# A third quad per gate/up block, silu in one ScalarE pass, and turned blocks carried by DMA in an RWKV-7 macaron block

## The chip, the core and the metric

The kernel runs on one core of one Trainium2 chip. A core has TensorE (PE in the profile; its weight loads are PEld), VectorE (DVE), ScalarE (ACT), GpSimd (POOL) and SyncE (SP), each with a queue of its own that it works through in order, and 16 DMA engines. The metric is the time on the device of one execution, in microseconds; before the change it is 2059.87 us, the median of three runs (2057.18 to 2060.95).

## The reference

One block on 256 tokens of width 2048, in float32: a gated feed-forward network (FFN), a mixer, a second FFN, each with a norm before and after and a residual. The change lies in the two FFNs; of the mixer only that it lies between them matters here.

```python
D_MODEL = 2048
SEQ = 256
D_FF = int(math.ceil(8 * D_MODEL / 3 / 256)) * 256      # 5632
MACARON_WEIGHT = 0.5
...
def _swiglu(x, w_gate, w_up, w_down):
    return (jax.nn.silu(x @ w_gate) * (x @ w_up)) @ w_down
...
    for l in range(DEPTH):
        f = _swiglu(_rmsnorm(h, ln_ffn1_pre[l]), ffn1_gate[l], ffn1_up[l], ffn1_down[l])
        h = h + MACARON_WEIGHT * _rmsnorm(f, ln_ffn1_post[l])
        mx = _hybrid_mixer(_rmsnorm(h, ln_mix_pre[l]), w_in[l], rwkv_mu[l], rwkv_w0[l],
...
        h = h + _rmsnorm(mx, ln_mix_post[l])
        f = _swiglu(_rmsnorm(h, ln_ffn2_pre[l]), ffn2_gate[l], ffn2_up[l], ffn2_down[l])
        h = h + MACARON_WEIGHT * _rmsnorm(f, ln_ffn2_post[l])
```

## The kernel before

*Products in two parts.* TensorE multiplies in a rounded float32 (F32R). To keep float32's accuracy every operand is split into a high part (the rounded value) and a low part (the rest), and a product is three matmuls into one PSUM bank: high x high, low x high, high x low (`mm3`, L173 to L175). Weights come as 128 x 1024 tiles `w32` by SP's DMAs; ScalarE's cast makes the high part `wH` (L149, in quads L379), VectorE's subtraction the low part `wL` (L150, in quads L380). There are four buffers for `w32` (`W32_BUFS`) and five for each of `wH` and `wL` (`WS_BUFS`): a split waits for TensorE to be through with the fifth tile before it, and a load for the splits of the fourth tile before it.

*Tiles.* The 256 tokens are two halves of 128 rows. Gate and up are computed in 11 blocks of 512 columns; each sums over 2048 inputs, 16 slices of 128 called k, two of which make a k pair. A pair of one weight is 4 products, 12 matmuls of 512 columns. Down has four blocks of 512 columns over 44 k.

*Quads.* Blocks 2 to 10 of each FFN (`FAST`) and down use `seven`. It takes two weights together: with the token halves as rows, the two slices of a k pair in the middle and the two weights (gate and up; in down two column blocks) as columns, a k pair is a 2 x 2 by 2 x 2 block product of 8 products. A quad forms it with seven, from sums of inputs (`sums`, made once per FFN as soon as the inputs stand) and from sums of weights that VectorE makes for each quad: `t13` (two differences, L367), then `t24` (L372 and L373, each reading the one before). Four splits follow: `a` and `b` of loaded tiles, `t13`, and `t24`; `a`, `t13` and `t24` hold two products each, `b` one. Before the change two of the eight k pairs of a fast block are quads (`n` = 2, after the fifth gate pair and the second up pair: `((4,), (1,))`), the other six are plain pairs for gate and for up. When the last quad is done, `merge` adds its banks up in VectorE (a copy on ScalarE, L401, and six additions, L404).

*Gate and up together.* `ev_f` then has ScalarE form the sigmoid of the gate's result u into a PSUM bank that has come free (L636), and VectorE multiply u by it (L638): that is silu. At the end of a block `finish` (L414) adds the up result of one half, `ev_l` (L642) multiplies it with the silu, and `turn` (L568) transposes it in VectorE in 32 x 32 squares into a tile `T1`; then the same for the other half. In the plain blocks 0 and 1 `ev_g` and `ev_gm` do silu by a sigmoid and a VectorE product (L653).

*Carrying a turned block.* Down needs the hidden values with the columns on the partitions. The transposed squares must still move between groups of 32 partitions: `carry_at` does that in the next block with 16 ScalarE copies of 32 x 256 (L594), 0.9 us apart on the clock of the hand-written order, and splits the result into high (L598) and low parts (L602).

*The order.* ScalarE, VectorE and TensorE run in an order written out by hand: `put` appends TensorE's steps with their length on a model clock, and `at` sets other work at a time of that clock; `slot` gives the time when one of the five split buffers comes free. What stands in a queue is not overtaken: an operation that waits holds up all behind it. SP and POOL take their instructions as the scheduler places them.

Of the kernel before, what the change touches and what calls it, by code (L numbers as in the profile page):

```python
# [18 lines left out]
P = 128  # L19
D = 2048  # L20
S = 256
# [27 lines left out]
FAST = range(2, 11)  # L49

# [5 lines left out]
class Block:  # L56
# [195 lines left out]
    def sums(s, T, out, when, own=None):  # L252
# [6 lines left out]
        def first():  # L259
            xH, xL = T[len(out) // 2]  # L260
            x = tt["x"] = s.unit((P, 2, 2, S), F32, "sx")
            V.tensor_tensor(out=fl(x), in0=xH.bitcast(F32).rearrange("p k t -> p (k t)"),
                            in1=xL.bitcast(F32).rearrange("p k t -> p (k t)"), op=ALU.add)

        def second():
            x = tt["x"]
            a11, a21 = x[:, :, 0, :P], x[:, :, 0, P:]
            a12, a22 = x[:, :, 1, :P], x[:, :, 1, P:]
            f = tt["f"] = s.unit((P, 4, 2, P), F32, "sf")
# [32 lines left out]
        def third():  # L302
            tt["H"], tt["L"] = [s.unit((P, 4, 2, P), F32R, n_) for n_ in ("sH", "sL")]
            nc.scalar.copy(fl(tt["H"]), fl(tt["f"]))

        def fourth():
            f, fH, fL = tt["f"], tt["H"], tt["L"]
            V.tensor_tensor(out=fl(fL), in0=fl(f), in1=fl(fH).bitcast(F32), op=ALU.subtract)
            for i in range(2):
                out.append([(fH[:, m, i], fL[:, m, i]) for m in range(4)])  # L310
# [4 lines left out]
    def seven(s, wf, cf, wl, cl, at, KT, T, sm, n, spots, ev_first, ev_last, trail=False):  # L315
# [35 lines left out]
        def quad(q):  # L351
# [18 lines left out]
            def t24():  # L370
                o = v["t24"]
                V.tensor_tensor(out=o[:, 0], in0=v["a"][:, 0], in1=v["t13"][:, 1], op=ALU.add)  # L372
                V.tensor_tensor(out=o[:, 1], in0=v["b"][:, 0], in1=o[:, 0], op=ALU.subtract)  # L373
# [22 lines left out]
        def merge():  # L396
# [12 lines left out]
            s.at(m + 4, lambda: ev_first(0, u[1], bank["p1"]))  # L409
            s.at(m + 4.6, lambda: ev_first(1, u[3], bank["p6"]))  # L410

        def finish(h):
            o = u[2 * h]
            V.tensor_tensor(out=o, in0=bank[f"l{h}"], in1=o, op=ALU.add)  # L414
            ev_last(h, o)
# [10 lines left out]
        if trail:  # L426
            s.by_half(wl, cl, stop, KT, s.clk, AHEAD[0],
                      lambda k, h: mul(f"l{h}", rows(k, h), ws[k]), keep, finish)
            return
# [136 lines left out]
    def turn(s, T1, h, src):  # L566

        s.nc.vector.transpose(out=T1[:, h * 512:h * 512 + 512], in_=src)  # L568

    def shuffle_split(s, T1, T, j):  # L570

        nc = s.nc
        x32 = s.unit((P, 4, S), F32, "x32")
        src = T1.rearrange("p (h k j c) -> p h k j c", h=2, k=4, j=4)
        dst = x32.rearrange("p k (h i c) -> p h k i c", h=2, i=4)
        for i in range(4):
            for q in range(4):
                nc.scalar.copy(dst[q * 32:q * 32 + 32, :, :, i],
                               src[i * 32:i * 32 + 32, :, :, q])
        dH, dL = T[j]  # L580
        nc.scalar.copy(dH, x32)
        nc.vector.tensor_tensor(out=dL, in0=x32, in1=dH.bitcast(F32), op=ALU.subtract)

    def carry_at(s, T1, T, t):
# [4 lines left out]
        def one(i, q):  # L589
            src = T1[0].rearrange("p (h k j c) -> p h k j c", h=2, k=4, j=4)  # L590
            if not x:
                x.append(s.unit((P, 4, S), F32, "x32"))
            dst = x[0].rearrange("p k (h i c) -> p h k i c", h=2, i=4)
            nc.scalar.copy(dst[q * 32:q * 32 + 32, :, :, i], src[i * 32:i * 32 + 32, :, :, q])  # L594

        def high():
            T.extend(s.new_T(1))
            nc.scalar.copy(T[-1][0], x[0])  # L598

        def low():  # L600
            dH, dL = T[-1]
            nc.vector.tensor_tensor(out=dL, in0=x[0], in1=dH.bitcast(F32), op=ALU.subtract)  # L602
# [8 lines left out]
    def ffn(s, wg, wu, wd, uT, rs, gpost, resid, emit, reload, xs=None):  # L611
# [7 lines left out]
        def block(b):  # L619
# [8 lines left out]
            def ev_g(h, ps):  # L628
                sg = s.tmp("sg")
                nc.scalar.activation(out=sg, in_=ps, func=AF.Sigmoid, scale=rs[h])  # L630
                nc.vector.scalar_tensor_tensor(out=sg, in0=ps, scalar=rs[h], in1=sg,
                                               op0=ALU.mult, op1=ALU.mult)
                sig[h] = sg

            def ev_f(h, u, free):
                nc.scalar.activation(out=free, in_=u, func=AF.Sigmoid)  # L636
                sig[h] = u
                s.at(s.now + 1.2, lambda: nc.vector.tensor_tensor(  # L638
                    out=u, in0=u, in1=free, op=ALU.mult))

            def ev_l(h, o):
                nc.vector.tensor_tensor(out=o, in0=o, in1=sig[h], op=ALU.mult)  # L642
                turned(h, o)

            def ev_gm(h, ps):
                sg = s.tmp("sg")
                nc.scalar.activation(out=sg, in_=ps, func=AF.Sigmoid, scale=r[h])
                sig[h] = sg
                s.at(s.now + 1.2, lambda: nc.vector.scalar_tensor_tensor(
                    out=sg, in0=ps, scalar=r[h], in1=sg, op0=ALU.mult, op1=ALU.mult))  # L650
# [27 lines left out]
            s.gemm_at(wg, b * 512, x, NKD, ev_gm)  # L678
# [40 lines left out]
    def post(s, wd, at, KT, gpost, fac, resid, emit, reload, hT=None, sm=None):  # L719
# [52 lines left out]
        if hT is not None:  # L772
# [3 lines left out]
            for c in (0, 2):  # L776
                ev = ev_of(c)
                s.seven(wd, c * 512, wd, c * 512 + 512, at, KT, hT, sm, NQ[c == 2], QUADS[c == 2],
                        lambda h, u, _, ev=ev: ev(h, u), ev_of(c + 1), c == 2)
# [761 lines left out]
```

## Time and profile before

| | us |
|---|---|
| median of three runs | 2059.87 |
| lowest and highest | 2057.18, 2060.95 |
| the profiled execution | 2060.43 |
| its span, first to last instruction | 2058.7 |
| TensorE busy in the span | 2043.5 |
| VectorE busy | 1687.5 |
| ScalarE busy | 1247.4 |
| POOL busy | 76.0 |

The blocks are found by the transposes of L568, two per block: those of the first FFN's blocks start between 58.2 and 485.0 us, those of the second's between 1398.6 and 1824.3. The second FFN's down projection follows to the end; between the first FFN's down projection and 1398.6 lie the mixer and the second FFN's first block.

How to read the rows: "busy" is the union of an engine's instructions; the number in brackets is their count. A row of the timeline has the start, the length, engine, line, operation and shapes, a count when like instructions are merged, and in brackets the idle time before it with what ended it. Rows of grouped instructions have the count, the busy time, the mean of one in nanoseconds, and the idle time before them. A matmul's length in the trace overlaps the next one's; its pace is read from start to start.

### The profile page before, as it was taken

Reading aid. Unit: us, or ns where it says so; the run is one execution under the profiler, and the core shown is the slowest. Engines: PE = TensorE matmul, PEld = TensorE weight load, DVE = VectorE, ACT = ScalarE, POOL = GpSimd, SP = SyncE. Lnnn points to the kernel's source line nnn. Section 1 sums busy time; section 2 is a strip of 40 time slices with the busy share of each in tenths; the row PEclk is TensorE's granted clock in tenths of the full one; section 3 lists DMA queues with packets and bytes.
Section 4 is the critical chain, followed back from the end, with each engine's and each line's share of the span. In section 5 each row is a group of like instructions: output and inputs, shape, how many; then the busy total and the mean of one; then the engine's idle time right before and its main releaser. Section 6 shows DMA issues by size and latency. Waiting matters only on the chain.

```text
span 2058.7 us, 29579 instructions
## 1 busy us (share of the span) xinstructions
PE 2043.5 (99%) x10901; PEld 1721.7 (84%) x10901; DVE 1687.5 (82%) x2188; ACT 1247.4 (61%) x1788; POOL 76.0 (4%) x161
## 2 busy tenths in 40 slices
PE   9999999999999999999999999999999999999998
PEld 7888888888888899999888888888888888888886
DVE  6898889888988865799688667578988898889886
ACT  7667666776555574474465444466677666765553
POOL 0000000000000000000110110010000000000000
PEclk9999999999999999999999999999999999999999
DMA  7566666665667766656456565665666666656674
GB/s 259 175 195 211 194 206 194 196 212 176 210 208 251 228 189 187 180 159 196 133 155 193 161 245 189 205 211 169 203 199 200 214 195 194 197 186 215 210 254 155
DMA packets 226170, 407.03 MB, mean 198 GB/s; under 512 B 15199, under 2 KB 51177, under 8 KB 226025
## 3 DMA queue, kind: packets, MB, share of 16 engines
q1 hardware_dynamic: 219849, 384.69, 59.7%
q0 software_dynamic: 5888, 19.93, 2.7%
q8 instruction: 85, 1.39, 0.3%
q10 hardware_dynamic: 288, 0.52, 0.1%
q14 instruction: 60, 0.49, 0.1%
HBM read 396.69 MB, written 8.39 MB: 197 GB/s over the span
## 4 chain that ended last, share of the span: by engine, by line
PE 92%; DVE 3%; issue 2%; DMA 2%; ACT 1%; POOL 0%; POOLq 0%; DVEq 0%; SPq 0%; ACTq 0%
PE mm L173 24%; PE mm L175 23%; PE mm L174 23%; PE mc L523 10%; PE ms L175 3%; PE ms L173 3%; PE ms L174 3%; DMA w<-in_ffn_down_dram 1%; DVE wL L150 1%; PE tr L551 1%; ACT x L594 0%; PE pA L1262 0%; ACT wH L149 0%; DVE u L404 0%; ACT wH L379 0%
## 5 line engine op out<-in xcount | busy, mean ns | idle before, releaser
L150 DVE TENSOR_TENSOR wL<-w,wH 128x1024 fp32r<-128x1024 f32 (+2 forms) x597 | 711.4, 1206 | 232.9 <-ACT wH L149 229.9
L149 ACT CAST wH<-w 128x1024 fp32r<-128x1024 f32 (+2 forms) x597 | 614.8, 1043 | 392.4 <-PE mm L175 200.5
L173 PE MATMUL mm<-wH,xH 128*128 128x512 f32 x2076 | 811.6, 392 | 0.0
L175 PE MATMUL mm<-wH,xL 128*128 128x512 f32 x2076 | 808.5, 389 | 0.7 <-DVE xL L559 0.5
L174 PE MATMUL mm<-wL,xH 128*128 128x512 f32 x2076 | 808.4, 389 | 0.7 <-DVE wL L150 0.7
L175 PEld LDWEIGHTS mm<-wH,xL 128*128 128x128 f32 x2076 | 389.7, 188 | 82.8 <-DVE xL L559 1.5
L174 PEld LDWEIGHTS mm<-wL,xH 128*128 128x128 f32 x2076 | 389.8, 188 | 81.2 <-DVE wL L150 1.6
L173 PEld LDWEIGHTS mm<-wH,xH 128*128 128x128 f32 x2076 | 389.6, 188 | 81.0 <-ACT xH L557 0.2
L379 ACT CAST wH<-t 128x1024 fp32r<-128x1024 f32 x128 | 134.5, 1052 | 72.7 <-DVE t L367 42.6
L380 DVE TENSOR_TENSOR wL<-t,wH 128x1024 fp32r<-128x1024 f32 x128 | 152.5, 1218 | 25.0 <-ACT wH L379 25.0
L379 ACT CAST wH<-w 128x1024 fp32r<-128x1024 f32 (+1 forms) x128 | 107.2, 838 | 96.7 <-PE mm L175 51.6
L523 PE MATMUL mc<-xH,wH 128*128 128x256 f32 x560 | 159.5, 285 | 0.0
L523 PE MATMUL mc<-xL,wH 128*128 128x256 f32 x560 | 158.4, 283 | 0.0
L523 PE MATMUL mc<-xH,wL 128*128 128x256 f32 x560 | 158.4, 283 | 0.0
L594 ACT COPY x<-T 32x256 f32<-32x256 f32 x352 | 142.2, 404 | 10.9 <-DVE T L568 4.6
L380 DVE TENSOR_TENSOR wL<-w,wH 128x1024 fp32r<-128x1024 f32 (+1 forms) x128 | 116.7, 950 | 1.3 <-ACT wH L379 1.3
L523 PEld LDWEIGHTS mc<-xH,wH 128*128 128x128 f32 x560 | 106.0, 189 | 1.1
L523 PEld LDWEIGHTS mc<-xH,wL 128*128 128x128 f32 x560 | 106.0, 189 | 0.2
L523 PEld LDWEIGHTS mc<-xL,wH 128*128 128x128 f32 x560 | 106.0, 189 | 0.1
L367 DVE TENSOR_TENSOR t<-w,w 128x1024 f32<-128x1024 f32 x64 | 78.0, 1218 | 16.4 <-DMA w<-in_ffn_down_dram 12.0
L174 PE MATMUL ms<-wL,sH 128*128 128x512 f32 x164 | 63.8, 389 | 0.0
L175 PE MATMUL ms<-wH,sL 128*128 128x512 f32 x164 | 63.8, 389 | 0.0
(298 smaller groups left out, 1974.7 us busy)
## 6 DMA issues: line engine op xcount, KB each, us to landing
w<-in_ffn_up_dram SPq DMA_DIRECT2D x140, 512.0 KB
w<-in_ffn_gate_dram SPq DMA_DIRECT2D x138, 512.0 KB
w<-in_w_in_dram SPq DMA_DIRECT2D x128, 512.0 KB
w<-in_ffn_down_dram SPq DMA_DIRECT2D x120, 512.0 KB
w<-in_ffn_down_dram SPq DMA_DIRECT2D x112, 256.0 KB
w<-in_ffn_gate_dram SPq DMA_DIRECT2D x76, 256.0 KB
w<-in_ffn_up_dram SPq DMA_DIRECT2D x72, 256.0 KB
w<-in_w_out_dram SPq DMA_DIRECT2D x32, 512.0 KB
```

The lines of the kernel that those rows point to most:

```text
L149: s.nc.scalar.copy(vH, v)
L150: s.nc.vector.tensor_tensor(out=vL, in0=v, in1=vH.bitcast(F32), op=ALU.subtract)
L173: nc.tensor.matmul(ps, aH, bH, start=start, stop=False)
L174: nc.tensor.matmul(ps, aH, bL, start=False, stop=False)
L175: nc.tensor.matmul(ps, aL, bH, start=False, stop=stop)
L367: V.tensor_tensor(out=v["t13"], in0=v["a"], in1=v["b0"].to_broadcast([P, 2, 512]), op=ALU.subtract)
L379: nc.scalar.copy(H, v[n_])
L380: V.tensor_tensor(out=L, in0=v[n_], in1=H.bitcast(F32), op=ALU.subtract)
L523: s.nc.tensor.matmul(o, lh, rh, start=one and n == 0, stop=k == KT - 1 and n == 2, skip_group_check=True)
L551: nc.tensor.transpose(ps[:, i], src[:, i * P:(i + 1) * P], s.ident)
L594: nc.scalar.copy(dst[q * 32:q * 32 + 32, :, :, i], src[i * 32:i * 32 + 32, :, :, q])
```

## The change

- `NG, SPOTS`: a fast block has three quads, after the third and fifth gate pairs and after the second up pair, and five plain pairs for each of gate and up. The sums of inputs for the third k pair are formed in block 1 (`nq=1`, both parts in one tile).
- In every quad, down's too, `t24` is two separate operations: `split("a")` comes between `t13` and the first, `split("b")` between the first and the second.
- In `merge` the order of the six additions changes by one place; at the end of a fast block (`one_end`) both totals, both products and both transposes stand in that order, no longer one half after the other.
- Silu is one ScalarE pass (`AF.Silu`), in place in fast blocks and from PSUM in blocks 0 and 1; the VectorE products are gone.
- `turn` writes its squares in another order, so that `carry_at` can move each of 16 pieces as 32 runs of 1 KB: 16 DMAs issued by POOL take the place of the 16 copies. The splits are made in two halves, the first cast 10 us after the carry's time, the second 13 (`CARRY`), each low part 2 us later.

```diff
+CARRY = (10, 13)
+NG, SPOTS = 3, ((2, 4), (1,))
...
-    def sums(s, T, out, when, own=None):
+    def sums(s, T, out, when, own=None, nq=2):
...
-            xH, xL = T[len(out) // 2]
-            x = tt["x"] = s.unit((P, 2, 2, S), F32, "sx")
-            V.tensor_tensor(out=fl(x), in0=xH.bitcast(F32).rearrange("p k t -> p (k t)"),
-                            in1=xL.bitcast(F32).rearrange("p k t -> p (k t)"), op=ALU.add)
+            xH, xL = [t[:, :2 * nq].bitcast(F32).rearrange("p k t -> p (k t)")
+                      for t in T[len(out) // 2]]
+            x = tt["x"] = s.unit((P, 2, 2, S), F32, "sx")[:, :nq]
+            V.tensor_tensor(out=fl(x), in0=xH, in1=xL, op=ALU.add)
...
-            tt["H"], tt["L"] = [s.unit((P, 4, 2, P), F32R, n_) for n_ in ("sH", "sL")]
+            if nq == 1:
+                u = s.unit((P, 2, 4, 1, P), F32R, "sHL")
+                tt["H"], tt["L"] = u[:, 0], u[:, 1]
+            else:
+                tt["H"], tt["L"] = [s.unit((P, 4, nq, P), F32R, n_) for n_ in ("sH", "sL")]
...
-            def t24():
-                o = v["t24"]
-                V.tensor_tensor(out=o[:, 0], in0=v["a"][:, 0], in1=v["t13"][:, 1], op=ALU.add)
-                V.tensor_tensor(out=o[:, 1], in0=v["b"][:, 0], in1=o[:, 0], op=ALU.subtract)
+            def t2():
+                V.tensor_tensor(out=v["t24"][:, 0], in0=v["a"][:, 0], in1=v["t13"][:, 1],
+                                op=ALU.add)
+
+            def t4():
+                V.tensor_tensor(out=v["t24"][:, 1], in0=v["b"][:, 0], in1=v["t24"][:, 0],
+                                op=ALU.subtract)
...
-            for t, fn in ((a, get), (a, t13), (a, t24), (a, lambda: split("a", 2)),
-                          (b, lambda: split("b", 1)), (c, lambda: split("t13", 2)),
+            for t, fn in ((a, get), (a, t13), (a, lambda: split("a", 2)), (a, t2),
+                          (b, lambda: split("b", 1)), (b, t4), (c, lambda: split("t13", 2)),
                           (d, lambda: split("t24", 2))):
...
-            for j, a in enumerate(((1, "p6", 0), (2, "p7", 1), (3, "p5", 2), (1, "p5", 1),
+            for j, a in enumerate(((1, "p6", 0), (2, "p7", 1), (1, "p5", 1), (3, "p5", 2),
                                    (1, "f0", 1), (3, "f1", 3))):
...
+        def total(h):
+            V.tensor_tensor(out=u[2 * h], in0=bank[f"l{h}"], in1=u[2 * h], op=ALU.add)
...
+        def both():
+            total(0)
+            total(1)
+            ev_last((u[0], u[2]))
...
-        s.nc.vector.transpose(out=T1[:, h * 512:h * 512 + 512], in_=src)
+        dst = T1.rearrange("p (j h k c) -> p h k j c", j=4, h=2, k=4)[:, h]
+        s.nc.vector.transpose(out=dst, in_=src.rearrange("p (k j c) -> p k j c", k=4, j=4))
...
-            nc.scalar.copy(dst[q * 32:q * 32 + 32, :, :, i], src[i * 32:i * 32 + 32, :, :, q])
...
+            x.append(s.unit((P, 4, 2, 4, 32), F32, "x32"))
+            src = T1[0].rearrange("p (j h k c) -> p j h k c", j=4, h=2, k=4)
+            for i in range(4):
+                for q in range(4):
+                    nc.gpsimd.dma_start(out=x[0][q * 32:q * 32 + 32, i],
+                                        in_=src[i * 32:i * 32 + 32, q])
...
-        for n in range(16):
-            s.at(t + 0.9 * n, lambda n=n: one(n // 4, n % 4))
-        s.at(t + 15, high)
-        s.at(t + 17, low)
+        s.at(t, move)
+        for h in range(2):
+            s.at(t + CARRY[h], lambda h=h: high(h))
+            s.at(t + CARRY[h] + 2, lambda h=h: low(h))
...
-            def ev_f(h, u, free):
-                nc.scalar.activation(out=free, in_=u, func=AF.Sigmoid)
+            def ev_f(h, u):
                 sig[h] = u
-                s.at(s.now + 1.2, lambda: nc.vector.tensor_tensor(
-                    out=u, in0=u, in1=free, op=ALU.mult))
-
-            def ev_l(h, o):
-                nc.vector.tensor_tensor(out=o, in0=o, in1=sig[h], op=ALU.mult)
-                turned(h, o)
...
+                nc.scalar.activation(out=u, in_=u, func=AF.Silu)
+
+            def ev_l(o):
+                for h in range(2):
+                    nc.vector.tensor_tensor(out=o[h], in0=o[h], in1=sig[h], op=ALU.mult)
+                for h in range(2):
+                    turned(h, o[h])
...
+                s.sums(st["nT"], st["su"], s.clk + 27, nq=1)
...
-                s.seven(wg, b * 512, wu, b * 512, s.T_at(nT), NKD, nT, su, 2, ((4,), (1,)),
-                        ev_f, ev_l)
+                s.seven(wg, b * 512, wu, b * 512, s.T_at(nT), NKD, nT, su, NG, SPOTS,
+                        ev_f, ev_l, one_end=True)
```

More of the change, by code (lines that the diff above doesn't have):

```diff
@@ L308, in fourth @@
             V.tensor_tensor(out=fl(fL), in0=fl(f), in1=fl(fH).bitcast(F32), op=ALU.subtract)
-            for i in range(2):
+            for i in range(nq):
                 out.append([(fH[:, m, i], fL[:, m, i]) for m in range(4)])
@@ L587, in carry_at, with move, by_k, part @@
         x = []
[L589 to L600, printed above, removed]
[L601 to L606 removed]
+        def move():
+            x.append(s.unit((P, 4, 2, 4, 32), F32, "x32"))
[4 more added lines that the diff above has]
+                                        in_=src[i * 32:i * 32 + 32, q])
+        def by_k(h):
+            return x[0][:, :, h].rearrange("p i k c -> p k i c")
+        def part(t_, h):
+            return t_[:, :, h * P:h * P + P].rearrange("p k (i c) -> p k i c", i=4)
+        def high(h):
+            if h == 0:
+                T.extend(s.new_T(1))
+            nc.scalar.copy(part(T[-1][0], h), by_k(h))
+        def low(h):
+            dH, dL = T[-1]
+            nc.vector.tensor_tensor(out=part(dL, h), in0=by_k(h),
+                                    in1=part(dH, h).bitcast(F32), op=ALU.subtract)
+        s.at(t, move)
+        for h in range(2):
+            s.at(t + CARRY[h], lambda h=h: high(h))
+            s.at(t + CARRY[h] + 2, lambda h=h: low(h))
     def sumsq(s, src, acc):
```

46 lines of the change are left out of this document (14 added, 32 removed).

## The prediction

> **What bounds the kernel now.** I read the totals and the chain that ended last first, then busy time by stage.
>
> ```profile
> span 2058.7 us, 29579 instructions
> PE 2043.5 (99%) x10901; PEld 1721.7 (84%) x10901; DVE 1687.5 (82%) x2188; ACT 1247.4 (61%) x1788; POOL 76.0 (4%) x161
> PE 92%; DVE 3%; issue 2%; DMA 2%; ACT 1%; POOL 0%; POOLq 0%; DVEq 0%; SPq 0%; ACTq 0%
> ```
>
> TensorE is the bound. A busy TensorE may still run slowly, so the stages matter. The first row below holds the gate/up blocks 1 to 10 of the first FFN, the second one fast block, the third the first down projection.
>
> ```profile
> core 0: us, PE busy (x) PEld busy (x) DVE busy (x) ACT busy (x) POOL busy (x), PEclk, DMA share, GB/s
> 101.00:482.00 381.00, 381.00 (x1683) 315.48 (x1682) 336.97 (x370) 261.68 (x362) 0.00 (x0) 1.00 0.63 200
> 225.20:267.40 42.20, 42.20 (x188) 34.95 (x187) 37.43 (x43) 28.96 (x40) 0.00 (x0) 1.00 0.63 200
> 483.00:700.00 217.00, 215.75 (x948) 177.25 (x947) 190.59 (x216) 124.74 (x153) 3.40 (x6) 1.00 0.68 218
> ```
>
> In the gate/up stage TensorE has no idle time at all, at clock 1.00; VectorE is busy 37.43 of 42.20 us (89%), ScalarE 28.96 (69%). Down loses 217.00 - 215.75 = 1.25 us. The pace of a matmul comes from the timeline of TensorE inside that block:
>
> ```profile
> 249.77 0.39 PE L173 MATMUL mm<-wH,xH 128*128 128x512 f32 x1
> ...
> 255.89 0.39 PE L173 MATMUL mm<-wH,xH 128*128 128x512 f32 x1
> ```
>
> From the first row to the last are 27 starts, across pairs and a quad alike: 6.12 / 27 = 0.2267 us each (the 0.39 is latency). So a block is 186 of these, and only fewer matmuls, or a new stall, change it.
>
> **The change, part by part.**
>
> *The third quad.* A quad makes seven products of three matmuls where two pairs make eight: 3 matmuls fewer in each of 18 blocks (9 per FFN), 54 x 0.2267 = **12.2 us**, if nothing starves TensorE. A block becomes 183 matmuls, 41.5 us. The price lies on VectorE, whose own pace the next view shows (the block's end; TensorE enters the next block at 267.45).
>
> ```profile
> 260.49 2.73 DVE L404 TENSOR_TENSOR u<-ms,u 128x512 f32<-128x512 f32 x4
> 263.26 1.29 DVE L404 TENSOR_TENSOR u<-mm,u 128x512 f32<-128x512 f32 x2
> 264.46 1.22 DVE L150 TENSOR_TENSOR wL<-w,wH 128x1024 fp32r<-128x1024 f32 x1
> 266.18 1.23 DVE L150 TENSOR_TENSOR wL<-w,wH 128x1024 fp32r<-128x1024 f32 x1 [0.51 <-ACT wH L149]
> 267.32 1.28 DVE L638 TENSOR_TENSOR u<-u,ms 128x512 f32<-128x512 f32 x2
> 268.52 1.22 DVE L150 TENSOR_TENSOR wL<-w,wH 128x1024 fp32r<-128x1024 f32 x1
> 269.66 0.68 DVE L414 TENSOR_TENSOR u<-mm,u 128x512 f32<-128x512 f32 x1
> 270.37 0.69 DVE L642 TENSOR_TENSOR u<-u,u 128x512 f32<-128x512 f32 x1
> 271.10 0.71 DVE L568 STREAM_TRANSPOSE T<-u 128x512 f32<-128x512 f32 x1
> 271.74 0.65 DVE L414 TENSOR_TENSOR u<-mm,u 128x512 f32<-128x512 f32 x1
> ```
>
> Start to start, 1024 columns cost 1.14 us (268.52 to 269.66) and 512 cost 0.60 (267.32 to 268.52 for two) when the next operation does not read the result: they overlap. Where it does (269.66, 270.37, 271.10) a step costs 0.72: 0.12 more. A quad adds t13 1.14, t2 and t4 1.20, and four low parts 3 x 1.14 + 0.60: 6.4 us, in place of two pairs' 2.3.
>
> *VectorE ops kept off their inputs.* Today a block has 11 such steps: 4 in its quads, 3 among the adds, 4 from total to product to transpose. After the change one is left (p6 to p7): 10 x 0.12 = 1.2 us saved. *Silu* removes two products (L638), 1.2 us. The block's VectorE sum is 37.4 + 6.4 - 2.3 - 1.2 - 1.2 = **39.1 of 41.5 us**, 94%. It fits; whether in time is the question below.
>
> *ScalarE* loses the 16 shuffles and gains a quad's casts:
>
> ```profile
> L149 ACT CAST wH<-w 128x1024 fp32r<-128x1024 f32 x12 | 12.4, 1052 | 4.7 <-DMA w<-in_ffn_gate_dram 2.3 <-PE mm L175 1.6 <-ACT x L594 0.4
> L594 ACT COPY x<-T 32x256 f32<-32x256 f32 x16 | 6.5, 404 | 0.4 <-DVE T L568 0.2
> L379 ACT CAST wH<-w 128x512 fp32r<-128x512 f32 x2 | 1.2, 622 | 1.7 <-DVE u L642 1.7
> L636 ACT ACTIVATE ms<-u 128x512 f32<-128x512 f32 x2 | 1.1, 602 | 2.6 <-DVE u L404 2.6
> 39.99 1.28 ACT L630 ACT_TABLE_LOAD   x1
> ```
>
> 28.96 - 6.5 + (3 x 1.05 + 0.62) - 2 x 1.05 = 24.1 us of 41.5. Silu itself no row shows; Sigmoid on the same shape takes 0.602, the old pair Sigmoid and product 1.2, and I take 0.6. Strided halves cost nothing extra by the L594 row: 256 columns in runs of 32 take 0.404, and 0.622 is 512 unbroken. The built order has two more table loads (before the mixer's first sigmoid, and at the second FFN's first silu): 1.28 each, behind ScalarE's idle third, 2.6 us if that cover were gone. Mixer and SP queue are otherwise the same; a third quad splits two weight DMAs into four (36 more in all), same bytes.
>
> *Block 1* also forms the third pair's sums, once per FFN.
>
> ```profile
> 60.00:101.00 41.00, 41.00 (x182) 33.95 (x182) 36.90 (x37) 28.34 (x39) 0.00 (x0) 1.00 0.56 166
> L262 DVE TENSOR_TENSOR sx<-xH,xL 128x1024 f32<-128x1024 f32 x10 | 12.2, 1218 | 0.0
> L653 DVE SCALAR_TENSOR_TENSOR sg<-mm,rs,sg 128x512 f32<-128x512 f32 x8 | 5.8, 726 | 0.0
> ```
>
> One addition of half L262's shape is 0.6; four combinations of 128 columns are at most 0.35 each (an estimate: 0.14 by the pace of 1.14 per 1024, and no more than 0.2 fixed); a low part is 0.6: 2.6 us more, less the block's two silu products (L653), 1.4: 38.1 of 41. It fits and costs nothing; 1 us per FFN if it comes late.
>
> *Is VectorE in time?* Let E be TensorE's entry into a block: three pairs (8.16), quad 0 (a 1.36, b 0.68, c and d 1.36 each), two pairs, quad 1, two pairs, quad 2, three pairs. In its queue VectorE has, ahead of quad 0's b: next block's pair 1, six adds, pair 2, t13, a, t2, then totals, products, transposes. Pair 1's weights wait for the fourth buffer back (up pair 2), whose cast waits for the fifth split buffer back, free 12.9 us before E. Cast and low part end at -10.4. From there the DMA:
>
> ```profile
> 254.54 1.54 SPq L135 DMA_DIRECT2D w<-in_ffn_gate_dram  x2
> 255.71 0.37 SPq L135 DMA_DIRECT2D w<-in_ffn_gate_dram  x1
> 258.26 1.05 ACT L149 CAST wH<-w 128x1024 fp32r<-128x1024 f32 x1 [1.80 <-DMA w<-in_ffn_gate_dram]
> 260.33 1.06 ACT L149 CAST wH<-w 128x1024 fp32r<-128x1024 f32 x1 [0.53 <-DMA w<-in_ffn_gate_dram]
> ```
>
> Issued at 254.54, usable at 258.26: 3.7 us; the next, 255.71 to 260.33: 4.6. So pair 1's low part is done at -4.4 (-3.5 with 4.6). Adds 3.7, pair 2, t13 and a 3.4, t2 0.6, six evacuations 3.7: the last transpose leaves at **E+7.0** (7.9). Then b and t4 1.2, c 1.22: E+9.4 (10.3). TensorE wants c's low part at 8.16 + 1.36 + 0.68 + 0.23 = 10.4. **Spare: 1.0 us (0.1)**, the tightest place of the block. I cost it at nothing; the cover is the low parts made ahead.
>
> *Turned blocks by DMA.* POOL issues 16 DMAs of 32 KB as soon as the second transpose is done; nothing else is in its queue there. Nearest rows: an issue over 32 partitions, with its landing, and POOL's slowest issues:
>
> ```profile
> L1346 POOL DMA_DIRECT2D w<-in_rwkv_g_dram x8: 496/498/514, 971.3 to 1147.9; - x8
> DMA to landing us min/median/max: 2.5/2.7/4.1
> L736 POOL DMA_DIRECT2D gb<-in_ln_ffn_post_dram x4: 538/564/703, 563.6 to 1978.3; - x4
> ```
>
> 16 x 0.50 + 2.7 = 10.7, from E+7.0: 17.7. By the other ends, 16 x 0.70 + 4.1 from 7.9: 23.2. The first cast of the carried block stands in ScalarE's queue ahead of up pair 0, whose low part TensorE wants at 23.12 + 0.23; less 1.22, 1.05 and 0.6 it may start at **E+20.5**. Spare 2.8 us by the nearest row, 2.7 late by the far one. I take the near row, for its 32 partitions; cost nothing. Landing lanes are eight deep, and 8 x 0.50 = 4.0 exceeds 2.7, so no issue waits for one. In the last gate/up block of each FFN the carried data is wanted only late in the down projection.
>
> *Down.* Its quads get the same new order. In the first one TensorE is stalled by a split that stands behind t24:
>
> ```profile
> 519.37 0.39 PE L173 MATMUL ms<-wH,xH 128*128 128x512 f32 x1
> 520.15 0.50 PE L174 MATMUL ms<-wL,xH 128*128 128x512 f32 x1 [0.39 <-DVE wL L380]
> 516.28 1.23 DVE L367 TENSOR_TENSOR t<-w,w 128x1024 f32<-128x1024 f32 x1 [1.51 <-DMA w<-in_ffn_down_dram]
> 517.54 0.69 DVE L372 TENSOR_TENSOR t<-w,t 128x512 f32<-128x512 f32 x1
> 518.26 0.69 DVE L373 TENSOR_TENSOR t<-w,t 128x512 f32<-128x512 f32 x1
> ```
>
> 0.78 - 0.23 = 0.55 us lost. With a ahead of t2 and t4 its low part ends 1.4 us sooner, so I count -0.5; bounds are 0 and the stage's 1.25, and +1 if the fuller last block hands down less lead.
>
> **Sum:** 12.2 + 0.5 = 12.7. The profiled execution took 2060.43 us, 1.7 around its span, so 2047.7; the median shown, 2059.87, lies 0.56 lower: **2047.2 us**.
>
> **Rivals.**
>
> *Slower: the carry lands late.* Place: the first cast of the carried block. It decides once 16 issues and a landing exceed 20.5 - 7.0 = 13.5 us; every us beyond stalls ScalarE, then VectorE, then TensorE in each of 18 blocks. With 0.66 an issue and 4.1: 14.7 from E+7.5, 1.7 late, 31 us lost less 12.7: 2078. For: VectorE is 94% busy beside POOL and 512 KB more cross the DMA engines per block. Against: the down row has VectorE busy 190.59 of 217 while POOL's issues there took 0.54 to 0.70.
> The Trainium skill, "SBUF — State Buffer", section "Who interferes with whom", says that GpSimd cannot write descriptors while VectorE runs a two-port operation, but infers that a tensor_tensor, though it shares the read side, leaves them free. By that rule issues would stay short here, since nearly all these rows are TENSOR_TENSOR; that VectorE's load stretches an issue no run here shows.
>
> *Part given back: VectorE late at c.* Spare 0.1 with slow weight DMAs; with the overlap of 0.08 lost on the seven or so operations before it, c is 0.4 late: 18 x 0.4 = 7 us back, 2054. For: such DMAs are seen in every block. Against: the near row has 1.0.
>
> *No change:* 0.7 us of stall per block eats the gain exactly, 2060. It needs one of the above at just this size.
>
> **How the numbers follow.** Full gain 0.60 (2045 to 2050), part 0.14 (to 2055.7), no change 0.07, slower 0.19 (2064 to 2085). This kernel's measurement tells 0.2%, 4.1 us, from no change. Faster 0.74, same 0.07, slower 0.19. The range 2044.5 to 2063 leaves out the slower case and little else; the likeliest case's own is 2045 to 2050.
>
> **What would show it.** Right: fast blocks of 41.5 us with TensorE busy throughout, VectorE near 39 us, the window of ScalarE without copies near 24; carried casts not waiting for the DMA, or briefly; POOL issues near 0.5 us. Wrong: TensorE waiting for low parts of quad 0 (VectorE late), or ScalarE waiting 2 us and more on the carry each block, or POOL issues of 0.7 and landings over 4. What would make it wrong is chiefly the carry's 10.7 us.

## The result, and the profile after

| | kernel before | kernel after |
|---|---|---|
| median, us (5 runs each) | 2059.87 (2057.18 to 2060.95) | 2068.50 (2067.06 to 2069.88) |
| ratio, 95% interval | | 1.0044 [1.0031, 1.0056] |
| span of the profiled execution, us | 2058.7 | 2066.8 |

The changed kernel is slower by 0.44%; the prediction was 2047.2 us. First the totals of its page, then the same stages as before (one row more: the second FFN's gate/up stage).

```profile
span 2066.8 us, 30087 instructions
PE 2040.7 (99%) x10847; PEld 1711.0 (83%) x10847; DVE 1717.3 (83%) x2268; ACT 1126.4 (55%) x1498; POOL 248.9 (12%) x513
...
core 0: us, PE busy (x) PEld busy (x) DVE busy (x) ACT busy (x) POOL busy (x), PEclk, DMA share, GB/s
101.00:482.00 381.00, 376.61 (x1642) 307.74 (x1641) 349.57 (x400) 209.40 (x240) 70.56 (x144) 1.00 0.67 210
1443.00:1824.00 381.00, 374.01 (x1638) 305.73 (x1637) 348.00 (x398) 207.76 (x239) 70.56 (x144) 1.00 0.66 209
225.20:267.40 42.20, 42.08 (x186) 34.38 (x184) 39.99 (x47) 23.62 (x28) 7.84 (x16) 1.00 0.69 217
483.00:700.00 217.00, 216.85 (x956) 179.29 (x957) 191.48 (x221) 122.33 (x143) 11.15 (x22) 1.00 0.68 219
```

The matmuls are gone, 10901 less 10847, but TensorE now has holes where it had none. Before, it started 1683 matmuls in the first row's 381 us, now 1642; at 0.2267 us each that is 9.3 us lost. The second FFN's row falls short of the same 1683 by 45, 10.2 us. Together 19.5 us lost, against 12.2 gained and 1.1 won in the first down projection (0.15 us idle in the last row, 1.25 before): 6.2 us longer in these stages. The span grew by 8.1; the other 1.9 lies in the start and the blocks at the stages' ends. Part of it need not be the change's: over the first 60 us the granted clock was 0.97 in this execution, and 1.00 in those of the kernel before and of experiment 1.

What the holes wait for: TensorE's waits in the first FFN's fast blocks, then in the second's (us in total, times, longest).

```profile
PE mm L175 <- ACT wH L151: 1.9, 1, 1.9
PE mm L175 <- DVE u L414: 1.6, 3, 0.7
PE mm L176 <- DVE wL L152: 0.8, 1, 0.8
...
PE mm L175 <- DVE u L414: 4.5, 6, 1.3
PE mm L175 <- ACT wH L151: 1.6, 1, 1.6
PE mm L176 <- DVE wL L152: 0.9, 2, 0.8
```

There are two kinds. L414 is the merge: at a block's start TensorE wants the banks of f0 and f1, and the merge's last two additions have not read them yet. The other two lines are nearly all one large stall in each FFN. The two blocks that hold these stalls take 46.5 and 45.6 us from one pair of transposes to the next (401.46 to 447.96 and 1745.15 to 1790.73), where 183 matmuls need 41.5: some 9 of the 19.5 us. What keeps VectorE is seen in its own waits over five fast blocks (190 to 400 us), with ScalarE's wait for the carry:

```profile
DVE wL L152 <- ACT wH L151: 12.9, 10, 1.9
DVE wL L390 <- ACT wH L389: 0.3, 1, 0.3
ACT xH L613 <- DMA x<-T: 3.7, 5, 1.6
```

VectorE stands twice in each block, 2.6 us a block, at a weight's low part (L152) whose high part ScalarE has not made. The timeline of one block shows both places. TensorE enters the block with the first row. The others come from four answers: VectorE, GpSimd, ScalarE, VectorE again.

```profile
267.58 0.39 PE L175 MATMUL mm<-wH,xH 128*128 128x512 f32 x1
...
273.03 1.28 DVE L654 TENSOR_TENSOR u<-u,u 128x512 f32<-128x512 f32 x2
274.23 1.29 DVE L589 STREAM_TRANSPOSE T<-u 128x512 f32<-128x512 f32 x2
...
276.07 7.84 POOL L601 DMA_DIRECT2D x<-T  x16 [33.70 <-issue]
...
288.21 0.62 ACT L613 CAST xH<-x 128x512 fp32r<-128x512 f32 x1 [1.58 <-DMA x<-T]
288.74 2.00 ACT L151 CAST wH<-w 128x1024 fp32r<-128x1024 f32 x2
...
285.39 2.50 DVE L390 TENSOR_TENSOR wL<-t,wH 128x1024 fp32r<-128x1024 f32 x2
289.81 2.36 DVE L152 TENSOR_TENSOR wL<-w,wH 128x1024 fp32r<-128x1024 f32 x2 [1.92 <-ACT wH L151]
```

First place: ScalarE waits for the carry's DMAs until 288.21. Behind its cast in the queue stands the next weight's high part, and behind that, on VectorE, the low part: VectorE is idle 1.92 us. Second place, 16 us later (VectorE, TensorE, and the cast on ScalarE that VectorE waited for):

```profile
305.70 1.23 DVE L152 TENSOR_TENSOR wL<-w,wH 128x1024 fp32r<-128x1024 f32 x1 [1.43 <-ACT wH L151]
306.84 2.73 DVE L414 TENSOR_TENSOR u<-ms,u 128x512 f32<-128x512 f32 x4
309.49 1.28 DVE L414 TENSOR_TENSOR u<-mm,u 128x512 f32<-128x512 f32 x2
...
309.20 0.39 PE L177 MATMUL mm<-wH,xL 128*128 128x512 f32 x1
310.32 0.47 PE L175 MATMUL mm<-wH,xH 128*128 128x512 f32 x1 [0.73 <-DVE u L414]
...
304.61 1.05 ACT L151 CAST wH<-w 128x1024 fp32r<-128x1024 f32 x1 [1.90 <-DMA w<-in_ffn_gate_dram]
```

VectorE stands 1.43 us at another low part, with the six additions queued behind it. They end after 310, and TensorE's next block begins at 310.32 instead of 309.43: 0.9 us lost, for operands it does not lack, only banks. This second wait does not come from the carry: ScalarE's cast stood 1.90 us for the weight's own load. The kernel before has such a wait at the same place (1.80 us at 258.26, a row of the prediction).

The large stall is in the next-to-last block of each FFN (VectorE, GpSimd, ScalarE):

```profile
401.46 1.29 DVE L589 STREAM_TRANSPOSE T<-u 128x512 f32<-128x512 f32 x2
...
406.23 5.39 POOL L601 DMA_DIRECT2D x<-T  x11 [37.67 <-ACT wH L151]
...
418.42 0.62 ACT L613 CAST xH<-x 128x512 fp32r<-128x512 f32 x1 [4.56 <-DMA x<-T]
...
1753.68 3.92 POOL L601 DMA_DIRECT2D x<-T  x8 [2.60 <-issue]
```

In the first FFN the first issue comes 3.5 us after the last transpose (402.75), not 0.5; ScalarE stands 4.56 us, and behind it VectorE's low part and TensorE. The last row is of the second FFN: there the first issue is in time (1746.98, 0.5 us after the last transpose), but GpSimd pauses 2.60 us after the eighth, and ScalarE stands 4.21 us, until 1761.77.

### The profile page after: what moved, and what is told of

The parts are those of the page before. It is cut to its first block, busy times and chain, and to the rows that moved or that the text cites. A ratio compares the mean times of both kernels' runs of the same rounds, so it can differ in the third digit from the quotient of the medians.

```text
span 2066.8 us, 30087 instructions
## 1 busy us (share of the span) xinstructions
PE 2040.7 (99%) x10847; PEld 1711.0 (83%) x10847; DVE 1717.3 (83%) x2268; ACT 1126.4 (55%) x1498; POOL 248.9 (12%) x513
## 5 line engine op out<-in xcount | busy, mean ns | idle before, releaser
L152 DVE TENSOR_TENSOR wL<-w,wH 128x1024 fp32r<-128x1024 f32 (+2 forms) x561 | 664.8, 1206 | 238.6 <-ACT wH L151 234.5
L175 PE MATMUL mm<-wH,xH 128*128 128x512 f32 x1968 | 772.1, 393 | 10.8 <-DVE u L414 7.1
L176 PE MATMUL mm<-wL,xH 128*128 128x512 f32 x1968 | 767.9, 390 | 2.2 <-DVE wL L152 2.2
L177 PE MATMUL mm<-wH,xL 128*128 128x512 f32 x1968 | 768.0, 390 | 0.2 <-DVE xL L579 0.2
L151 ACT CAST wH<-w 128x1024 fp32r<-128x1024 f32 (+2 forms) x561 | 572.8, 1041 | 355.0 <-PE mm L177 168.9
L389 ACT CAST wH<-t 128x1024 fp32r<-128x1024 f32 x164 | 172.7, 1053 | 275.2 <-DVE t L382 189.8
L601 POOL DMA_DIRECT2D x<-T x352 | 172.8, 499 | 755.8 <-issue 381.0
L390 DVE TENSOR_TENSOR wL<-t,wH 128x1024 fp32r<-128x1024 f32 x164 | 198.4, 1219 | 8.8 <-ACT wH L389 5.4
L390 DVE TENSOR_TENSOR wL<-w,wH 128x1024 fp32r<-128x1024 f32 (+1 forms) x164 | 155.4, 947 | 1.3 <-ACT wH L389 1.3
L175 PE MATMUL ms<-wH,sH 128*128 128x512 f32 x164 | 64.0, 390 | 0.0
```

Of the source, the lines that this page charges most:

```text
L151: s.nc.scalar.copy(vH, v)
L152: s.nc.vector.tensor_tensor(out=vL, in0=v, in1=vH.bitcast(F32), op=ALU.subtract)
L175: nc.tensor.matmul(ps, aH, bH, start=start, stop=False)
L176: nc.tensor.matmul(ps, aH, bL, start=False, stop=False)
L177: nc.tensor.matmul(ps, aL, bH, start=False, stop=stop)
L389: nc.scalar.copy(H, v[n_])
```

## The experiments

The first four test where the merge's lateness comes from, with the large stall beside it; the others test what fills VectorE. Ratios are to the kernel before, run on the same chip.

**1. Two quads again.** The other three parts of the change stay.

```diff
-NG, SPOTS = 3, ((2, 4), (1,))
+NG, SPOTS = 2, ((4,), (1,))
...
-                s.sums(st["nT"], st["su"], s.clk + 27, nq=1)
```

> The changed kernel with two quads in each gate/up block at the old spots, and without the sums for a third; the one-pass silu, the carry by DMAs, the new order of VectorE's operations and the merge's new order stay. Theory M (the third quad's loads on VectorE push the merge's additions past the next block's start, so that TensorE waits for the banks of f0 and f1): those waits (0.8 to 1.7 us before the next block's first product in most fast blocks of the changed kernel) are gone, TensorE is at its own pace in the fast blocks, and the time is that of the kernel before or a little less (down's lost 1.2 us each come back): 2056 to 2061 us. Rival C (the DMA carry's late landings are what TensorE pays for): the high halves of the carried block still come late, waits of TensorE stay, and the time stays above that of the kernel before, 2063 to 2068 us.

2058.38 us, 0.9994 [0.9985, 1.0004]. TensorE is busy 381.00 of the 381.00 us of the first gate/up stage, though the carry is the same. So silu, carry and order together make no difference that can be measured with two quads, and the loss needs the third. VectorE's waits in five fast blocks of this kernel (190 to 400 us) show why:

```profile
DVE wL L152 <- ACT wH L151: 21.5, 20, 1.5
DVE wL L390 <- ACT wH L389: 7.5, 5, 1.5
DVE t L374 <- DMA w<-in_ffn_gate_dram: 0.9, 3, 0.4
```

It waits 29.9 us, more than twice as long as in the changed kernel, and TensorE loses nothing by it: VectorE has that time to spare.

**2. More room in the unit pool, 3. the additions in another order, 4. both.** Units are the SBUF buffers of one shared pool, from which the carry takes its target too. In experiment 2 down's six units are taken only when its evacuation starts; in 3 the additions of f0 and f1 come third and fourth:

```diff
-            for j, a in enumerate(((1, "p6", 0), (2, "p7", 1), (1, "p5", 1), (3, "p5", 2),
-                                   (1, "f0", 1), (3, "f1", 3))):
+            for j, a in enumerate(((1, "p6", 0), (2, "p7", 1), (1, "f0", 1), (3, "f1", 2),
+                                   (1, "p5", 1), (3, "p5", 3))):
...
-        gb = [s.unit(p="gb") for _ in range(2)]
-        fg = [[s.unit(p="fg") for _ in range(2)] for _ in range(2)]
+        gb, fg = [None, None], [[None, None], [None, None]]
...
+                if c % 2 == 0:
+                    fg[h][c // 2] = s.unit(p="fg")
                 if h == 0 and c % 2 == 0:
+                    gb[c // 2] = s.unit(p="gb")
```

> The changed kernel, with the six units that the down projection's evacuation needs (gb, fg) taken from the unit pool when that evacuation starts and not before the eleven blocks. Theory U (the late first issue of the carry in each FFN's next-to-last block, 3.5 us late at 406.2 us, comes from a pool of units that is used up): the wait of ScalarE's xH for the carry, 4.6 and 4.2 us there, falls under 2 us, the half-speed clock after it (3.4 us at 421.4) goes too, and the kernel is 8 to 11 us shorter than the changed one, 2057 to 2061 us. Rival C (the DMAs land late whatever the units do): the two stalls and the time stay, 2066 to 2070 us.

> The changed kernel with the merge's six additions in another order: the two that read the banks of f0 and f1 third and fourth, the two that read p5's bank last. Same sums, same count. Theory M (TensorE stands at the next block's start until the additions of f0 and f1 have read their banks): both banks come free two additions, some 1.2 us, sooner, most of the waits of 0.8 to 1.7 us at the block starts go, and the kernel is 7 to 12 us shorter than the changed one, 2057 to 2062 us. Rival V (VectorE has no time left in a fast block, so that any order only moves the wait): the waits turn up at the weight pairs or at p5's bank instead, and the time stays within 3 us of the changed kernel's, 2066 to 2070 us.

> The changed kernel with both of the last two edits: the down projection's units taken late, and the additions of f0 and f1 third and fourth in the merge. Theories M and U together: the two losses are of different blocks and add, 15 to 21 us less than the changed kernel, 2047 to 2053 us, near what 54 fewer matmuls at 0.2267 us each make of the kernel before (2047.6). Rival V or C: 2060 us or more.

2068.37, 2068.20 and 2067.50 us, 1.0040 [1.0026, 1.0054], 1.0040 [1.0025, 1.0055], 1.0038 [1.0025, 1.0051]: no change, and both of my first theories fell. In 2 the longest wait for the carry is 4.8 us still. In 3 the waits for the banks are gone from the list of TensorE's waits in the first FFN, and others stand in their place:

```profile
PE mm L175 <- ACT wH L151: 2.1, 1, 2.1
PE ms L176 <- DVE wL L390: 2.0, 4, 0.6
PE mm L176 <- DVE wL L152: 1.5, 2, 0.8
```

A wait that only moves when its place is mended suggests that the engine behind it, VectorE, has no time left. That left the question of what fills it: work, or waits.

**5. The carried block's casts later on ScalarE.** One constant. The DMAs leave when they did; the cast that waits for them stands four places further back in ScalarE's queue, behind the weight casts.

```diff
-CARRY = (10, 13)
+CARRY = (15, 18)
```

> The changed kernel with the carried block's high halves asked for 5 us later on ScalarE (CARRY 15 and 18 in place of 10 and 13), behind the weight casts that now stand behind them. Theory Q (VectorE needs 39 us of a 41.5 us block, and loses 2.6 us more to waits for a weight's high part; about half of that wait is ScalarE standing at the carried block's high half, whose DMAs land late, with the next weight cast queued behind it): ScalarE's waits for the carry nearly go, the two stalls of 4.8 and 4.0 us in each FFN's next-to-last block go or fall under 1 us, VectorE's idle per block falls by about 1.2 us, and the kernel is 9 to 16 us shorter than the changed one, 2052 to 2059 us. Rival V (VectorE's work alone fills the block): only the two stalls go, 2059 to 2062 us.

2047.00 us, 0.9942 [0.9926, 0.9959]: 21.5 us less than the changed kernel. The first gate/up stage, and the same place of the block at 265 as shown above (ScalarE, VectorE):

```profile
101.00:482.00 381.00, 381.00 (x1682) 315.76 (x1681) 361.75 (x412) 217.16 (x245) 72.99 (x150) 1.00 0.67 214
...
283.87 1.05 ACT L151 CAST wH<-w 128x1024 fp32r<-128x1024 f32 x1 [0.49 <-PE mm L177]
287.86 0.62 ACT L613 CAST xH<-x 128x512 fp32r<-128x512 f32 x1
...
284.96 2.59 DVE L152 TENSOR_TENSOR wL<-w,wH 128x1024 fp32r<-128x1024 f32 x2 [0.31 <-ACT wH L151]
```

The cast of the carry waits for nothing now, and the weight casts that VectorE needs next stand ahead of it. The large stalls are gone too: ScalarE's longest wait for the carry is 0.3 us.

**6. The merge earlier, 7. both.** In 6 the merge's copy and additions move ahead of one weight pair; CARRY is as in the changed kernel. In 7 CARRY is 15 and 18 besides.

```diff
-            s.at(m + 0.2, start)
+            s.at(m - 1.0, start)
...
-                s.at(m + 0.7 + 0.1 * j, lambda a=a: add(*a))
+                s.at(m - 0.9 + 0.1 * j, lambda a=a: add(*a))
```

> The changed kernel with the merge's copy and six additions placed 1.2 to 1.6 us earlier in program order, ahead of one more weight cast and its low part (the additions keep their order). Theory Q: VectorE no longer stands 1.1 us at a low part whose cast waits for a slot with the additions queued behind it; the waits of 0.8 to 1.7 us at the block starts go, the two stalls of the next-to-last blocks stay: 2058 to 2062 us. Rival V: the waits move to other places, 2066 to 2070 us.

> Both of the last two edits together. Theory Q: VectorE's idle per block is under 0.8 us, TensorE keeps its own pace in the fast blocks, and the time is near what 54 fewer matmuls at 0.2267 us each make of the kernel before, 2045 to 2051 us. Rival V: 2058 us or more.

6: 2051.39 us, 0.9962 [0.9947, 0.9977]. ScalarE waits for the carry no less than before the edit (4.7 us in the five blocks, 3.7 before), and yet TensorE keeps its pace in all fast blocks but the next-to-last, since the second of VectorE's two waits is gone. The gain, 17 us, is larger than I had expected, for the large stall shrank as well: TensorE is busy 379.78 of the first stage's 381.00 us, 376.61 in the changed kernel, while ScalarE's longest wait is still 4.8 us. My reading, which no run isolates, is that a VectorE that is not behind has low parts made ahead. So in an ordinary block either edit alone, the cast later or the merge earlier, brings TensorE's pace back: each of VectorE's two waits can be borne, and both together cannot. 7: 2048.95 us, 0.9952 [0.9938, 0.9967], as expected, and no better than 5. The earlier merge acts on the down projections too; at the ends of both, TensorE waits 1.0 and 1.8 us for weight splits (`kH`, `kL`), and not at all in experiment 5.

**8. The old carry.** Plain transposes and ScalarE's sixteen copies, from the kernel before, with three quads (diff: `turn` and `carry_at` as in the kernel before).

> The changed kernel with the old carry: the plain transposes, and sixteen copies of 32 partitions on ScalarE per block in place of the sixteen DMAs; three quads, the one-pass silu and VectorE's new order stay. Theory Q (the DMAs' late landings cost VectorE some 1.2 us a block and the two stalls of 4 to 5 us): no wait of ScalarE for a DMA of the carry, so the stalls go, but the copies (some 0.3 us each, 5 us a block) and the one high part of 128x1024 come back on ScalarE, which has the room: 2054 to 2062 us. Rival S (ScalarE's copies stand ahead of weight casts as the waits did, and delay VectorE as much): 2064 to 2072 us.

2084.19 us, 1.0121 [1.0106, 1.0136]: slower than either theory had it, on the side of rival S. VectorE waited 18.5 us for ScalarE in the five blocks' 210 us. That ScalarE's copies (404 ns each, not the expected 0.3 us) delay the weight casts behind them, as the waits do, fits this and was not tested apart; neither were the copies at other places in the order. At their old places the third quad does not pay with them.

**9. Two us later instead of five.**

```diff
-CARRY = (10, 13)
+CARRY = (12, 15)
```

> The changed kernel with the carried block's high halves asked for 2 us later (CARRY 12 and 15), which puts the first of them behind the next two weight casts. Theory Q (the cost is the weight cast queued on ScalarE behind a high half that waits for a late DMA): nearly all of the gain of 5 us later comes at once, 2046 to 2051 us, since the casts that VectorE needs next no longer stand behind it; where the stall of the next-to-last block stays in part, up to 2055. Rival W (it is the DMA's lateness itself, some us for each us): about two fifths of the way, 2058 to 2062 us.

2047.97 us, 0.9943 [0.9928, 0.9958]. Nearly all of the gain at once: what decides is the place in the queue, behind two more weight casts, and not the length of the delay.

**10. The old silu, 11. the old order, both on the kernel of experiment 5.** These put back, one at a time, what the prediction had priced at 1.2 us of VectorE in a block (the silu in the plain blocks 0 and 1 as well).

```diff
-                nc.scalar.activation(out=u, in_=u, func=AF.Silu)
+                nc.scalar.activation(out=free, in_=u, func=AF.Sigmoid)
...
+                s.at(s.now + 1.2, lambda: nc.vector.tensor_tensor(
+                    out=u, in0=u, in1=free, op=ALU.mult))
```

```diff
-            for t, fn in ((a, get), (a, t13), (a, lambda: split("a", 2)), (a, t2),
-                          (b, lambda: split("b", 1)), (b, t4), (c, lambda: split("t13", 2)),
+            for t, fn in ((a, get), (a, t13), (a, t24), (a, lambda: split("a", 2)),
+                          (b, lambda: split("b", 1)), (c, lambda: split("t13", 2)),
...
-            for j, a in enumerate(((1, "p6", 0), (2, "p7", 1), (1, "p5", 1), (3, "p5", 2),
+            for j, a in enumerate(((1, "p6", 0), (2, "p7", 1), (3, "p5", 2), (1, "p5", 1),
```

(and total, product and transpose of each half after each other again).

> The kernel with the high halves 5 us later (2047.0 us), with the sigmoid and its product on VectorE again in place of the one-pass silu. VectorE's idle there was 6.3 us in five blocks, 1.3 us in each, and the two products come to 1.2 us: by the prediction's step (silu buys 1.2 us of VectorE in a block) the spare is used up, some block starts wait again, 2047 to 2056 us. Rival N (the spare is larger than the idle shows, since a wait elsewhere shrinks): 2046 to 2048 us, no change.

> The kernel with the high halves 5 us later (2047.0 us), with VectorE's old order: t24's two halves back to back behind t13, the old order of the merge's additions, and each half's total, product and transpose after each other. By the prediction's step (ten dependent neighbours at 0.12 us each, 1.2 us of VectorE in a fast block) the spare of 1.3 us is used up: 2047 to 2056 us. Rival N: 2046 to 2048 us, no change.

2055.93 us, 0.9982 [0.9973, 0.9991], and 2055.60 us, 0.9985 [0.9976, 0.9994]: 8.9 and 8.6 us more than experiment 5, at the upper end of the range. Matmuls and carry are those of experiment 5; what is added is time on VectorE, and it costs that.

**12. The best of these.** CARRY as in 5, and the earlier merge in the gate/up blocks alone.

```diff
-            m = s.clk
+            m = s.clk - (1.2 if one_end else 0)
...
-                s.at(m + 0.7 + 0.1 * j, lambda a=a: add(*a))
...
+                s.at(m + (0.3 if one_end else 0.7) + 0.1 * j, lambda a=a: add(*a))
```

> The kernel with the high halves 5 us later, and the merge's copy and additions 1.2 to 1.6 us earlier in the gate/up blocks alone (the down projection keeps its places, since the earlier merge there cost TensorE 3 to 4 us at the ends of both down projections). Theory Q: the fast blocks are at TensorE's pace already, so this gives more spare and no time: 2045 to 2048 us. Should the waits that are left hide something: 2042 to 2045.

2046.43 us, 0.9936 [0.9924, 0.9949]: faster than both kernels, and within the spread of experiment 5.

**VectorE's account.** Over the same 210 us of fast blocks (190 to 400 us), the stage row of experiment 1 and of the changed kernel (their waits were shown above), then row and waits of experiments 5, 10 and 11:

```profile
190.00:400.00 210.00, 210.00 (x928) 173.91 (x927) 177.61 (x200) 112.22 (x125) 37.42 (x77) 1.00 0.66 213
...
190.00:400.00 210.00, 208.45 (x913) 170.34 (x912) 195.87 (x225) 117.61 (x135) 39.19 (x80) 1.00 0.67 213
...
190.00:400.00 210.00, 210.00 (x928) 174.07 (x927) 200.55 (x228) 121.17 (x138) 38.89 (x80) 1.00 0.67 214
DVE wL L152 <- ACT wH L151: 6.3, 9, 1.1
DVE wL L390 <- ACT wH L389: 0.3, 1, 0.3
...
190.00:400.00 210.00, 209.31 (x918) 171.73 (x918) 202.97 (x237) 118.49 (x135) 39.07 (x80) 1.00 0.66 213
DVE wL L152 <- ACT wH L151: 5.8, 5, 1.3
DVE wL L390 <- ACT wH L389: 0.3, 1, 0.3
...
190.00:400.00 210.00, 209.48 (x918) 171.50 (x917) 200.73 (x227) 120.78 (x135) 39.09 (x80) 1.00 0.66 214
DVE wL L152 <- ACT wH L151: 6.6, 5, 1.4
```

The plain sum of VectorE's work and waits does not name the bound. It is 207.5 of 210 us in experiment 1, 209.1 in the changed kernel and 207.2 in experiment 5: an engine that is ahead spends its spare time in such waits too. What can be compared is the room that TensorE's own pace leaves beside VectorE's work, and the waits that have to fit in it. Per block (matmuls started in the row over 183, or 186 with two quads; TensorE's pace is 183 or 186 times 0.2267 us):

| kernel | VectorE's work, us | TensorE's pace, us | room | VectorE's waits | TensorE |
|---|---|---|---|---|---|
| 1, two quads | 35.6 | 42.2 | 6.6 | 6.0 | at its pace |
| changed kernel | 39.3 | 41.5 | 2.2 | 2.6 | behind |
| 5, casts later | 39.5 | 41.5 | 2.0 | 1.3 | at its pace |
| 10, old silu | 40.5 | 41.5 | 1.0 | 1.2 | behind |
| 11, old order | 40.0 | 41.5 | 1.5 | 1.4 | behind |

Four of the five come out as they should. Experiment 11 does not (its waits include 0.3 us in the five blocks for a weight's load): by the account its waits just fit, and yet TensorE is behind, with 2.4 of VectorE's 210 us idle in gaps that the list of waits does not have (2.8 in experiment 5). That the old order costs 8.6 us is shown by its time; the account does not show how.

## Why the prediction was wrong, point by point

- *54 matmuls at 0.2267 us, 12.2 us.* Right. Experiment 5, in which nothing starves TensorE in the fast blocks, lies 12.3 us under the kernel before, down included (12.7 forecast with it).
- *VectorE needs 39.1 of 41.5 us; "it fits".* The work was nearly right: 39.5 a block in experiment 5. What failed is that I compared work alone with the block and put VectorE's waits at nothing. It also stood 2.6 us a block at high parts that ScalarE had not made, and the room was 2.0 to 2.2. With two quads 6.0 us of such waits are free, as experiment 1 shows; with three, what exceeds the room is paid.
- *The carry lands at E+17.7, may wait until E+20.5, "cost nothing".* This is the step that failed, together with the waits left out above. In the block shown, E is 267.58. The transposes end at E+7.9, at my far end, the 16 issues take 7.84 us as predicted, and the cast starts at 288.21, E+20.6, since the last landing takes over 4 us where I took 2.7. Even so my limit is missed by just 0.1 us, and TensorE's next product is hardly late. But I set that limit by TensorE alone. Before it, the cast of the carry keeps the next weight's high part waiting on ScalarE, and that one VectorE, for 1.92 us. With the second wait of 1.43 us on top this is more than VectorE has, and TensorE pays 0.9 us at the end of the block. Taking the carry's wait away is worth 21.5 us, the large stalls included (experiment 5); taking the second away is worth 17.1 (experiment 6). Of the signs that I had named against this step only the landings over 4 us came (up to 6.1); issues stayed at 0.50, and ScalarE's waits on the carry are 0.7 us in an ordinary block, where I had asked for 2.
- *Quad 0's c the tightest place.* Wrong: the tightest is the merge's end, whose banks of f0 and f1 the next block's first products write. I had followed VectorE's queue for operands that TensorE reads and not for banks that it waits to have emptied.
- *The rival of a late carry* had the place and the chain (ScalarE, VectorE, TensorE) and the sign, but its condition, 13.5 us from the last transpose to the cast, was not met in the ordinary block shown: 288.21 - 275.52 = 12.7 us. It was met in the next-to-last block of the first FFN, 418.42 - 402.75 = 15.7 us. Its range, 2064 to 2085, holds the measured time, but partly by luck: it let TensorE stall 1.7 us in each of 18 blocks. The changed kernel started 15 matmuls fewer in the five ordinary blocks than experiment 5, 0.7 us a block, and lost more in two.
- *Silu and the order, 1.2 us of VectorE each.* Right in kind, shown by experiments 10 and 11; of VectorE's busy time they take 0.9 and 0.5 us a block (202.97 and 200.73 against 200.55 us, each over its own number of blocks). L650 took 0.633 us, predicted 0.6. The two more table loads cost nothing that can be seen.
- *ScalarE 24.1 us a block:* 23.62. *Block 1 fits:* yes, 45.30 us between the transposes of blocks 0 and 1 with TensorE busy for all of them. *Down:* -1.1 us of idle time in the first projection, near the far bound, where I took -0.5; nothing in the second (0.53 us idle in 210, 0.56 before).
- *Issues of 0.50 us.* Right: 498 ns beside a VectorE that is busy 39.99 of 42.20 us. The Trainium skill, "SBUF — State Buffer", section "Who interferes with whom", infers this for tensor_tensor operations, and the trace agrees. *No issue waits for a lane:* wrong, 12 did, 6.5 us in all.

```profile
L601 POOL DMA_DIRECT2D x<-T x352: 498/498/672, 62.1 to 1843.8; - x176
  DMA x<-T: 31.9, 20
  POOL x L601: 6.5, 12
DMA to landing us min/median/max: 1.7/3.5/6.1
```

ScalarE's casts waited for these DMAs 20 times in 44 (second row), 31.9 us in all; the third row is GpSimd's own wait for a lane.

Two things stay open. Why the landings reach 6 us is not settled; with two quads they reach 5.9. And why the carry of the next-to-last blocks is late: in the first FFN the profile puts the wait of its first issue down to a weight cast of ScalarE (L151), and giving the pool six units back did not change it; in the second FFN the pause of 2.60 us has no releaser in the profile.

## What to carry to other kernels

When a change fills an engine to some 95% of its block, set its waits, too, against the room that the bound engine's pace leaves: waits that were free while there was slack are paid as soon as they exceed it. A sum of work and waits near the whole time proves nothing by itself; take a wait out, or put some work back, and see whether the time follows. An operation that waits for a slow transfer belongs as far back in its in-order queue as its result allows, behind the work that a fuller engine waits for; here that one constant was worth 21 us. And when mending one wait only moves it, look for the engine with no time left and at what fills its time.

## What the runs showed of the hardware

The 32 KB transfers from SBUF to SBUF landed 1.7 to 6.1 us after their issue (median 3.5), beside the weights' loads, with the DMA engines busy 0.67 of the time in the fast blocks. The Trainium skill, "DMA: Bandwidth & Descriptors", section "Anatomy of one DMA — SWDGE (gpsimd) path", gives a fit of 2.0 us and bytes over 436 GB/s, which for 32 KB is 2.1 us (an estimate by that page). The fastest are near it; the median is not.

After the stall at 418 us TensorE ran at half its clock for about 3 us, after the like stall at 1761 us it did not (mean granted clock 0.57 and 1.00 in these 4 us); in experiment 2 it did after both.

```profile
421.00:425.00 4.00, 3.71 (x9) 2.93 (x10) 4.00 (x5) 2.69 (x4) 0.00 (x0) 0.57 0.64 183
1765.00:1769.00 4.00, 4.00 (x19) 3.31 (x18) 4.00 (x5) 2.33 (x4) 0.00 (x0) 1.00 0.75 245
```

The Trainium skill, "TensorE: Matmul & The Clock Gate", section "Part 1: The HAM clock gate", says that the clock is halved after an idle window of about 3.4 us, and that the window runs freely. By that a stall of about this length may or may not fill one. The rows do not contradict it, but do not show it either: TensorE started one matmul within each of these stalls, so neither was idle throughout.
